# Hymba-style decoder trunk: q and k of the differential attention projected channel-major, rotated rows moved by DMA

## The chip, the cores and the metric

One NeuronCore of a Trainium2 chip runs the kernel. TensorE (PE) does the matrix products, PEld is its weight load, VectorE (DVE), ScalarE (ACT) and GpSimd (POOL) do the rest, SyncE (SP) issues most DMAs. Times are device microseconds; the metric is the median time of a run. Beside the runs there is one execution taken by the profiler, and all rows below come from that one.

## What is computed

Two layers over 512 positions of width 1024, in float32. One projection of the normalised input gives ten parts of 512 columns; four mixers use them, each gated by its own part, and a second projection adds the result to x.

```python
for layer in range(DEPTH):                      # 2
    h = rms_norm(x, norm_g[layer])
    a_u, a_g, qd, kd, vd, b_g, c_x, c_g, m_q, m_g = split(h @ w_in[layer], 10)
    y_a = s5_mixer(a_u, ...)                    # diagonal complex state space, GELU, GLU
    q = rope_partial(qd.reshape(B, L, 4, 2, 64), cos, sin)   # rotates the first 16 of 64
    k = rope_partial(kd.reshape(B, L, 4, 2, 64), cos, sin)
    y_b = rms_norm(diff_attention(q, k, v, lam), da_subln_g[layer]) * (1 - lam_init)
    y_c = rglru_mixer(c_x, ...)                 # convolution of width 4, RG-LRU
    y_m = memory_attention(m_q, rms_norm(mem, mem_norm_g[layer]), w_mem_kv[layer])
    x = x + concat(y_a * silu(a_g), y_b * silu(b_g), y_c * silu(c_g), y_m * silu(m_g)) @ w_out[layer]
return rms_norm(x, final_norm_g)

def rope_partial(x, cos, sin):                  # half = 8
    x1, x2, xp = x[..., :8], x[..., 8:16], x[..., 16:]
    return concatenate([x1 * cos - x2 * sin, x2 * cos + x1 * sin, xp])
```

## The kernel before

Every projection matmul is done in three products of rounded halves: weights and inputs are split into hi and lo (`whi`, `wlo`, `hThi`, `hTlo`), and hi x hi, hi x lo and lo x hi are summed in PSUM. The weights come in pieces of 128 x 1024 by SyncE into two raw buffers; ScalarE casts each to `whi` (line 168) and VectorE subtracts it for `wlo` (line 174), three buffers each, asked for two pieces ahead of their use (`w_use`, line 178).

A projection runs in one of two layouts. `cm_block` (line 502) is channel-major: 256 columns at a time, the result has channels on the partitions and the 512 positions in the row; its matmuls stand at line 515. `tm_block` (line 522) is time-major: 512 columns, positions on the partitions; line 535. Either does 96 matmuls of 512 columns for a 512-column part, and yields after each 12 of them. Accumulators (`acc`) are four PSUM banks; a cm block takes two, a tm block four.

`ORDER` (line 30) gives the order of the projections of each layer. Between them run streams: generators that hold the other work (`params`, `s5_params`, `attention`, `lru`, `s5`, `mem_norm`, `mem_attention` and the ends of these). `Streams.tick` (line 77) is called at each yield of a projection; each stream whose due time has come then emits its next piece and says after how many ticks it is due again. So the program's order is written out by ticks, and it is the order of priority in which each engine takes instructions that are ready. A stream that needs another one polls it each tick.

What bears on the change:

- q and k are time-major. `qk_evac` (line 572) copies a 128-position tile out of PSUM into `qz` (line 575), rotates the first 16 of each 64 columns with four products and two sums on VectorE (`rab`, `qz`), and puts it on the list `pend`. Two ticks later `flush_qk` (line 589) turns it by four TensorE transposes (line 595) and copies it to `qT` (line 598), or for k splits it into `kT` (lines 603 and 604), one for each half of the head pairs, where own rows hold the hi part and the other rows the lo part.
- `attention` (line 608) starts when q, k and v are there (line 1266), `pend` is empty and `par` is done. It works through 16 items, four row blocks times four heads, one each `D_AT` = 2 ticks: scores (lines 645 and 646 on TensorE, the mask, the maximum at line 649, exponentials at line 655, and line 661 on VectorE), a tick pair later the transposes (669), two later the product with v (679). A row block's first item splits q into `qh` and `ql` (lines 629 to 632).
- Buffers come from pools with a fixed count of slots for each size: `big` (`b8`, 8 KB a partition, 14 slots: halves of h, q, the two kT, v, the memory's kv, the LRU's three, `au`, `U`, `yg`, the gates, `qm`), `sm2` (`b2`, 2 KB, 10 slots), `mid` (`b4`, 4 KB, 4 slots). A slot comes free when all uses of its tile are done, and the first write of the next tile waits for that.
- A gate's projection leaves PSUM by `gate_evac` (line 713): a tanh on ScalarE (716) and a product on VectorE (717) that writes the gate's `b8` tile.
- `lru_load` (line 1120) loads and splits the LRU's gate weights when cx is within `BD_AHEAD` entries of the plan; `mem_norm` starts when mk is within `MEM_AHEAD` = 2 entries (line 1151). In the plan a channel-major part has two entries, a time-major one one.
- At the end of a layer `gl` joins the S5 stream (line 1244), and the output projections (`oAM0` and on) join the others.

Of the kernel before, what the change touches and what calls it, by code (L numbers as in the profile page):

```python
# [9 lines left out]
F32 = mybir.dt.float32  # L10
# [6 lines left out]
P = 128  # L17
D = 1024
# [8 lines left out]
ROPE_THETA = 500000.0  # L27


ORDER = ["q v k kv cx au cg bg mq ag mg gl oAM0 oAM1 oBC0 oBC1".split(),  # L30
         "q k cx v kv au mq bg mg ag cg gl oAM0 oAM1 oBC0 oBC1".split()]

C_ID, C_DM, C_IF, C_KEEP, C_CM, C_END = 0, 128, 144, 152, 152, 280

# [13 lines left out]


MEM_AHEAD = 2  # L50
BD_AHEAD = 3
S5P_AT = 2
D_MEM = (3, 2, 1)
D_S5 = (1, 1, 2, 2, 1, 2)
D_AT = 2


class Streams:
# [31 lines left out]
def tile_kernel(ctx: ExitStack, tc: tile.TileContext, A, out):  # L90
# [26 lines left out]
    def b2(shape, name, dtype=F32):  # L117
        return sm2.tile(shape, dtype, tag="b2", name=nm(name))
# [10 lines left out]
    def tp(shape=(P, 4, 128)):  # L129
        return ps.tile(list(shape), F32, tag="tp", bufs=2, name=nm("tp"))  # L130
# [51 lines left out]


    xr = A["x"].rearrange("o (t p) d -> p (o t) d", p=P)
    xd = ctx.enter_context(tc.tile_pool(name="xd", bufs=1, space=bass.MemoryType.DRAM)).tile([L, D], F32, tag="xd", name="xd")
    xdr = xd.rearrange("(t p) d -> p t d", p=P)
    xt = {}

# [32 lines left out]
    for l in range(DEPTH):  # L221
        for n in ORDER[l]:
            if n == "kv":
                for u in range(2):
                    add(l, "mk", u, cm_pieces(A["w_mem_kv"][l], 256 * u))
                add(l, "mv", 0, tm_pieces(A["w_mem_kv"][l], 512))
            elif n == "gl":
                w = A["s5_w_glu"][l].rearrange("(k p) (s c) -> p k s c", p=P, s=2)
                for u in range(2):
                    add(l, "gl", u, [w[:, 2 * i:2 * i + 2, :, 256 * u:256 * u + 256] for i in range(2)])  # L230
            elif n[0] == "o":
                ps_ = []
                for g in n[1:3]:
                    r0 = 512 * "ABCM".index(g)
                    ps_ += tm_pieces(w_out[l, r0:r0 + 512], 512 * int(n[3]))
                add(l, "o", n[1:], ps_)
            elif n in ("q", "k", "v", "au"):
                add(l, n, 0, tm_pieces(w_in[l], COL[n]))
            else:
                for u in range(2):  # L240
                    add(l, n, u, cm_pieces(w_in[l], COL[n] + 256 * u))
# [107 lines left out]
    def tt(o, a, b, op):  # L349
        V.tensor_tensor(out=o, in0=a, in1=b, op=op)  # L350
# [63 lines left out]
    def params():  # L414
# [71 lines left out]
        V.tensor_scalar(out=cneg, in0=cpos, scalar1=-4.0, scalar2=None, op0=ALU.mult)  # L486
        V.tensor_scalar(out=cpos, in0=cpos, scalar1=4.0, scalar2=None, op0=ALU.mult)

    nsum = const.tile([P, NT], F32, tag="nsum", name="nsum")

    mrs = const.tile([P, 2], F32, tag="mrs", name="mrs")
# [77 lines left out]
        return ((lambda k, t: hi[k // 4][:, k % 4, t, :]), (lambda k, t: lo[k // 4][:, k % 4, t, :]))  # L569


    def qk_evac(dst):
        def f(t, a):
            z = b2([P, 8, 64], "qz")
            S.copy(z, a.rearrange("p (m d) -> p m d", d=64))
            z12 = z[:, :, 0:16].rearrange("p m (s f) -> p m s f", f=8)
            ca = rcos[:, t, :].unsqueeze(1).unsqueeze(1).to_broadcast([P, 8, 2, 8])
            sa = rsin[:, t, :].unsqueeze(1).unsqueeze(1).to_broadcast([P, 8, 2, 8])
            rab = b2([P, 2, 8, 2, 8], "rab")
            ra, rb = rab[:, 0], rab[:, 1]  # L580
            tt(ra, z12, ca, ALU.mult)
            tt(rb, z12, sa, ALU.mult)
            tt(z12[:, :, 0, :], ra[:, :, 0, :], rb[:, :, 1, :], ALU.subtract)
            tt(z12[:, :, 1, :], ra[:, :, 1, :], rb[:, :, 0, :], ALU.add)
            pend.append((dst, t, z, st.now))
        return f

    pend = []
    def flush_qk():

        while pend and st.now - pend[0][3] >= 2:
            dst, t, z, _ = pend.pop(0)
            pt = tp()
            for j in range(4):
                PE.transpose(pt[:, j, :], z[:, 2 * j:2 * j + 2, :].rearrange("p m d -> p (m d)"), ident)
            ts = slice(t * 128, (t + 1) * 128)
            if len(dst) == 1:
                S.copy(dst[0][:, :, ts], pt)
            else:

                for m in range(2):
                    own, oth = slice(m * 64, m * 64 + 64), slice(64 - m * 64, 128 - m * 64)
                    S.copy(dst[m][own, :, ts], pt[own])
                    tt(dst[m][oth, :, ts], pt[own], dst[m][own, :, ts], ALU.subtract)

    st.hook = flush_qk

    def attention(l, R):
        while pend or "par" in st.live:
            yield  # L610
        qT, kT, v = R["qT"][0], R["kT"], R["v"]
        o = qT
        R["o"] = o
        oss = const.tile([P, 16], F32, tag="oss", name=nm("oss"))
# [530 lines left out]
        st.start("s5p", s5_params(l, Rl[l]))  # L1145

    st.start("par", params())
    s5p_start(0)
    for pi, (l, n, u, ids) in enumerate(plan):
        R = Rl[l]  # L1150
# [5 lines left out]
        if any(p[0] == l and p[1] == "cx" for p in plan[pi:pi + BD_AHEAD]) and "bd" not in R:  # L1156
            lru_load(l, R)
        if n in ("q", "k"):
            R[n + "T"] = [b8([P, 4, L], "qT")] if n == "q" else [b8([P, 4, L], "kT", F32R) for _ in range(2)]
            run(tm_block(h_tm(), qk_evac(R[n + "T"]), ids))  # L1160
        elif n == "v":
            vt = R["v"] = b8([P, NT, 512], "v")

# [78 lines left out]
        elif n == "gl":  # L1242
# [4 lines left out]
            for hf, pid in enumerate(ids):  # L1247
                whi, wlo = (w.rearrange("p (k s c) -> p k s c", k=2, s=2) for w in w_use(pid))
                for j in range(2):
# [13 lines left out]
                        ag = R["ag"][:, 2 * u + j, :]  # L1263
                        V.scalar_tensor_tensor(out=ag, in0=th, scalar=0.25, in1=ag, op0=ALU.mult, op1=ALU.mult)
                    st.tick()
        if n in ("q", "k", "v") and all(a in R for a in ("qT", "kT", "v")):
            st.start("attn", attention(l, R))
        if n == "o":
            pair, half = u[:2], int(u[2])
# [99 lines left out]
```

## Time and profile before

| | before |
|---|---|
| median of 3 runs | 910.19 us (909.8 to 910.3) |
| the profiled execution | 911.01 us |
| its span, first to last instruction | 909.2 us |
| TensorE matmul busy | 887.7 us, 98% |
| TensorE weight load busy | 746.5 us, 82% |
| VectorE busy | 667.3 us, 73% |
| ScalarE busy | 510.7 us, 56% |
| GpSimd busy | 42.2 us, 5% |
| HBM read | 84.40 MB |

Busy times are unions of an engine's instructions. Matmuls overlap, so the distance from one start to the next says more than the duration of one. "Idle before" is the time an engine waited ahead of an instruction, with the one that ended the wait.

### The profile page before, as it was taken

How to read it: one execution, taken by the hardware profiler on the slowest of the kernel's cores; microseconds unless marked ns; L12 is line 12 of the kernel's file. 1: busy time of each engine (PE TensorE's matmuls, PEld its weight loads, DVE VectorE, ACT ScalarE, POOL GpSimd, SP SyncE). 2: the span in 40 equal slices, each digit the busy share in tenths (PEclk: the TensorE clock that was granted, in tenths of full speed). 3: DMA queues.
4: the chain of work that ended last, by engine and by line, in shares of the span. 5: the costliest groups of instructions: out<-in, count | busy, mean ns of one | idle time of the engine just before them, and what ended most of it. 6: DMA issues, size and time to landing. Idle time of an engine off the chain costs nothing.

```text
span 909.2 us, 12391 instructions
## 1 busy us (share of the span) xinstructions
PE 887.7 (98%) x4478; PEld 746.5 (82%) x4478; DVE 667.3 (73%) x1345; ACT 510.7 (56%) x1032; POOL 42.2 (5%) x86
## 2 busy tenths in 40 slices
PE   7999999999999999999999999999999999999996
PEld 5788878987878888888888888898888888788885
DVE  5984988778999956883384676875999996666343
ACT  5673786985344265921454468766656354863133
POOL 1001000001101100000100000000101110000000
PEclk9999999999999999999999999999999999999998
DMA  5743432022212236433343321432112222152322
GB/s 179 180 139 105 140 95 88 29 68 58 89 55 66 74 115 194 132 107 108 107 157 101 92 88 58 136 116 70 50 48 74 74 74 93 47 186 96 109 73 93
DMA packets 80929, 90.05 MB, mean 99 GB/s; under 512 B 23778, under 2 KB 58211, under 8 KB 80868
## 3 DMA queue, kind: packets, MB, share of 16 engines
q1 hardware_dynamic: 77842, 85.72, 30.1%
q10 hardware_dynamic: 722, 2.36, 0.8%
q0 software_dynamic: 2304, 1.18, 0.5%
q8 instruction: 35, 0.57, 0.3%
q14 instruction: 26, 0.21, 0.1%
HBM read 84.40 MB, written 4.19 MB: 97 GB/s over the span
## 4 chain that ended last, share of the span: by engine, by line
PE 73%; DVE 20%; ACT 5%; issue 2%; DMA 1%; SPq 0%; DVEq 0%; ACTq 0%
PE acc L535 38%; PE acc L515 16%; PE acc L1255 5%; DVE wlo L174 3%; DVE u L350 2%; DVE xr L1040 2%; DVE wt L350 2%; DVE xr L350 1%; PE ms L679 1%; PE tp L315 1%; PE sc L807 1%; PE sc L645 1%; PE tp L832 1%; PE sc L646 1%; DVE li L757 1%
## 5 line engine op out<-in xcount | busy, mean ns | idle before, releaser
L174 DVE TENSOR_TENSOR wlo<-raw,whi 128x1024 fp32r<-128x1024 f32 x136 | 166.0, 1221 | 120.8 <-ACT whi L168 117.0
L168 ACT CAST whi<-raw 128x1024 fp32r<-128x1024 f32 x136 | 143.2, 1053 | 190.4 <-PE acc L535 119.2
L515 PE MATMUL acc<-hThi,whi 128*128 128x512 f32 x384 | 153.3, 399 | 0.0
L515 PE MATMUL acc<-hThi,wlo 128*128 128x512 f32 x384 | 150.8, 393 | 0.0
L515 PE MATMUL acc<-hTlo,whi 128*128 128x512 f32 x384 | 150.6, 392 | 0.0
L535 PE MATMUL acc<-whi,hThi 128*128 128x512 f32 x256 | 104.1, 407 | 2.3 <-ACT whi L168 2.3
L535 PE MATMUL acc<-wlo,hThi 128*128 128x512 f32 x256 | 101.9, 398 | 0.0
L535 PE MATMUL acc<-whi,hTlo 128*128 128x512 f32 x256 | 101.1, 396 | 0.0
L535 PE MATMUL acc<-wlo,mxh 128*128 128x512 f32 x256 | 100.1, 391 | 0.0
L535 PE MATMUL acc<-whi,mxl 128*128 128x512 f32 x256 | 100.1, 391 | 0.0
L535 PE MATMUL acc<-whi,mxh 128*128 128x512 f32 x256 | 100.0, 391 | 0.0
L515 PEld LDWEIGHTS acc<-hThi,wlo 128*128 128x128 f32 x384 | 72.2, 188 | 14.8
L515 PEld LDWEIGHTS acc<-hTlo,whi 128*128 128x128 f32 x384 | 72.3, 188 | 13.3
L515 PEld LDWEIGHTS acc<-hThi,whi 128*128 128x128 f32 x384 | 72.2, 188 | 13.3
L535 PEld LDWEIGHTS acc<-whi,hThi 128*128 128x128 f32 x256 | 56.3, 220 | 10.3 <-ACT whi L168 2.7
L535 PEld LDWEIGHTS acc<-whi,hTlo 128*128 128x128 f32 x256 | 56.5, 221 | 7.8 <-DVE hTlo L318 0.2
L535 PEld LDWEIGHTS acc<-wlo,hThi 128*128 128x128 f32 x256 | 56.5, 221 | 7.2
L535 PEld LDWEIGHTS acc<-wlo,mxh 128*128 128x128 f32 x256 | 48.1, 188 | 9.8
L535 PEld LDWEIGHTS acc<-whi,mxl 128*128 128x128 f32 x256 | 48.1, 188 | 9.8
L535 PEld LDWEIGHTS acc<-whi,mxh 128*128 128x128 f32 x256 | 48.1, 188 | 9.6
L976 POOL DMA_DIRECT2D MT<-kq x64 | 32.1, 509 | 486.2 <-DVE kq L350 336.6
L655 ACT ACTIVATE e<-sc,nmx 128x128 f32<-128x128 f32 (+3 forms) x64 | 33.2, 528 | 10.3 <-DVE nmx L651 10.2
(313 smaller groups left out, 1643.1 us busy)
## 6 DMA issues: line engine op xcount, KB each, us to landing
raw<-in_w_in_dram SPq DMA_DIRECT2D x80, 512.0 KB, 3.6
raw<-in_w_out_dram SPq DMA_DIRECT2D x32, 512.0 KB, 3.4
raw<-in_w_mem_kv_dram SPq DMA_DIRECT2D x16, 512.0 KB, 3.3
x<-in_x_dram SPq DMA_DIRECT2D x8, 512.0 KB, 4.9
raw<-in_s_w_glu_dram SPq DMA_DIRECT2D x16, 256.0 KB, 3.2
mt<-in_mem_dram SPq DMA_DIRECT2D x4, 512.0 KB
xd<-x SPq DMA_DIRECT2D x4, 512.0 KB, 4.4
x<-xd SPq DMA_DIRECT2D x4, 512.0 KB, 5.5
```

The lines of the kernel that those rows point to most:

```text
L168: S.copy(hi, wbuf[j])
L174: V.tensor_tensor(out=lo, in0=raw, in1=hi, op=ALU.subtract)
L315: lastins["pe"] = PE.transpose(pt[:, k, :], h[:, kk * 128:(kk + 1) * 128], ident)
L350: V.tensor_tensor(out=o, in0=a, in1=b, op=op)
L515: PE.matmul(a[j][:, :ncol], w[:, kk, c], h(k), start=(hf == 0 and i == 0), stop=(hf == 1 and i == 3 * nh - 1))
L535: PE.matmul(a[t], h(k, t), w[:, kk, :], start=(p == 0 and kk == 0 and i == 0), stop=(p == np_ - 1 and kk == 1 and i == 2))
L645: PE.matmul(s[:, m, :M], qh[:, m, h, :], kT[m][:, h, :M], start=True, stop=False)
L646: PE.matmul(s[:, m, :M], ql[:, m, h, :], kT[m][:, h, :M], start=False, stop=True)
L655: S.activation(e[:, m, :N], s[:, m, :N], AF.Exp, bias=nmx[:, m:m + 1], scale=0.125, accum_out=sm[:, m:m + 1])
L976: G.dma_start(out=MT[g * 64 + 64 - n:g * 64 + 64, g, t], in_=kq[g * 64:g * 64 + n])
L1040: V.tensor_tensor_scan(out=xr_[i][:, j, :], data0=dec, data1=xr_[i][:, j, :], initial=0.0, op0=ALU.mult, op1=ALU.add)
L1255: PE.matmul(a, w[:, k, s, j * 128:(j + 1) * 128], h[:, 2 * hf + k, :], start=(hf == 0 and i == 0), stop=(hf == 1 and i == 5))
```

## The change

q and k are projected channel-major by `cm_block`, like the gates, and copied from PSUM as they are; no transposes follow. Their layout then has the 16 rotated channels of a 64-channel half on 16 partitions, for four head pairs. A new stream `rope` moves these rows by two DMAs of 128 KB into a tile of 128 partitions, where the two members of each rotated pair lie 32 partitions apart, rotates them with four products on 32 partitions and two instructions on 128, and moves them back by two DMAs. For k it then splits the tile into the two `kT`. The cosines and sines are needed in that layout too: `rope_tables` spreads them with eight GpSimd copies, turns them with eight TensorE transposes once, keeps them for layer 0 and stores them to DRAM, from where layer 1 loads them. k goes ahead of q in both layers, v ahead of both, and cx between k and q in layer 1. `attention` now waits for the streams `ropeq` and `ropek` and is started when q's projection ends; q's tile becomes its output tile as before. `D_ROPE` holds the ticks between the moves out and the rotation, and between the moves back and what follows, for each tensor and layer. `BD_AHEAD` goes from 3 to 1.

```diff
@@ -27,8 +27,8 @@
 ROPE_THETA = 500000.0
-ORDER = ["q v k kv cx au cg bg mq ag mg gl oAM0 oAM1 oBC0 oBC1".split(),
-         "q k cx v kv au mq bg mg ag cg gl oAM0 oAM1 oBC0 oBC1".split()]
+ORDER = ["v k q kv cx au cg bg mq ag mg gl oAM0 oAM1 oBC0 oBC1".split(),
+         "v k cx q kv au mq bg mg ag cg gl oAM0 oAM1 oBC0 oBC1".split()]
 C_ID, C_DM, C_IF, C_KEEP, C_CM, C_END = 0, 128, 144, 152, 152, 280
@@ -48,11 +48,12 @@
 MEM_AHEAD = 2
-BD_AHEAD = 3
+BD_AHEAD = 1
 S5P_AT = 2
 D_MEM = (3, 2, 1)
 D_S5 = (1, 1, 2, 2, 1, 2)
 D_AT = 2
+D_ROPE = {"k": ((2, 3), (2, 3)), "q": ((4, 6), (3, 5))}
 class Streams:
@@ -182,7 +183,8 @@
     xr = A["x"].rearrange("o (t p) d -> p (o t) d", p=P)
-    xd = ctx.enter_context(tc.tile_pool(name="xd", bufs=1, space=bass.MemoryType.DRAM)).tile([L, D], F32, tag="xd", name="xd")
+    dpool = ctx.enter_context(tc.tile_pool(name="xd", bufs=1, space=bass.MemoryType.DRAM))
+    xd = dpool.tile([L, D], F32, tag="xd", name="xd")
     xdr = xd.rearrange("(t p) d -> p t d", p=P)
     xt = {}
@@ -234,7 +236,7 @@
                     r0 = 512 * "ABCM".index(g)
                     ps_ += tm_pieces(w_out[l, r0:r0 + 512], 512 * int(n[3]))
                 add(l, "o", n[1:], ps_)
-            elif n in ("q", "k", "v", "au"):
+            elif n in ("v", "au"):
                 add(l, n, 0, tm_pieces(w_in[l], COL[n]))
             else:
                 for u in range(2):
@@ -486,6 +488,32 @@
         V.tensor_scalar(out=cneg, in0=cpos, scalar1=-4.0, scalar2=None, op0=ALU.mult)
         V.tensor_scalar(out=cpos, in0=cpos, scalar1=4.0, scalar2=None, op0=ALU.mult)
+    rtab = []
+    rtd = [dpool.tile([P, L], F32, tag=f"rtd{i}", name=f"rtd{i}") for i in range(2)]
+    def rope_tables():
+        for w, src in enumerate((rcos, rsin)):
+            rep_ = b2([P, NT, P], "rep")
+            for i in range(NT):
+                G.tensor_copy(rep_[:, i].rearrange("p (a f c) -> p a f c", a=4, c=4),
+                              src[:, i].unsqueeze(1).unsqueeze(3).to_broadcast([P, 4, 8, 4]))
+            yield 2
+            pr = tp()
+            for i in range(NT):
+                PE.transpose(pr[:, i, :], rep_[:, i], ident)
+            pf = pr.rearrange("p i c -> p (i c)")
+            tab = b2([P, L], f"rt{w}")
+            if w == 0:
+                S.copy(tab, pf)
+            else:
+                for g in range(4):
+                    r = slice(g * 32, g * 32 + 32)
+                    S.activation(tab[r], pf[r], AF.Copy, scale=-1.0 if g % 2 else 1.0)
+            rtab.append(tab)
+            G.dma_start(out=rtd[w], in_=tab)
     nsum = const.tile([P, NT], F32, tag="nsum", name="nsum")
     mrs = const.tile([P, 2], F32, tag="mrs", name="mrs")
@@ -569,46 +597,45 @@
         return ((lambda k, t: hi[k // 4][:, k % 4, t, :]), (lambda k, t: lo[k // 4][:, k % 4, t, :]))
-    def qk_evac(dst):
-        def f(t, a):
-            z = b2([P, 8, 64], "qz")
-            S.copy(z, a.rearrange("p (m d) -> p m d", d=64))
-            z12 = z[:, :, 0:16].rearrange("p m (s f) -> p m s f", f=8)
-            ca = rcos[:, t, :].unsqueeze(1).unsqueeze(1).to_broadcast([P, 8, 2, 8])
-            sa = rsin[:, t, :].unsqueeze(1).unsqueeze(1).to_broadcast([P, 8, 2, 8])
-            rab = b2([P, 2, 8, 2, 8], "rab")
-            ra, rb = rab[:, 0], rab[:, 1]
-            tt(ra, z12, ca, ALU.mult)
-            tt(rb, z12, sa, ALU.mult)
-            tt(z12[:, :, 0, :], ra[:, :, 0, :], rb[:, :, 1, :], ALU.subtract)
-            tt(z12[:, :, 1, :], ra[:, :, 1, :], rb[:, :, 0, :], ALU.add)
-            pend.append((dst, t, z, st.now))
-        return f
-    pend = []
-    def flush_qk():
-        while pend and st.now - pend[0][3] >= 2:
-            dst, t, z, _ = pend.pop(0)
-            pt = tp()
-            for j in range(4):
-                PE.transpose(pt[:, j, :], z[:, 2 * j:2 * j + 2, :].rearrange("p m d -> p (m d)"), ident)
-            ts = slice(t * 128, (t + 1) * 128)
-            if len(dst) == 1:
-                S.copy(dst[0][:, :, ts], pt)
-            else:
+    def rope(l, R, n):
+        z = R[n + "z"]
+        while "rtab" in st.live:
+            yield
+        if l and n == "k":
+            rtab[:] = [b2([P, L], f"rt{i}") for i in range(2)]
+            for w in range(2):
+                S.dma_start(out=rtab[w], in_=rtd[w])
+        x1, x2 = b2([P, L], "rx"), b2([P, L], "ry")
+        rows = [(x1[m * 64:m * 64 + 64], z[m * 64:m * 64 + 16]) for m in range(2)]
+        for x_, z_ in rows:
+            S.dma_start(out=x_, in_=z_)
+        yield D_ROPE[n][l][0]
+        co, si = rtab
+        for g in range(4):
+            to, fr = slice(g * 32, g * 32 + 32), slice((g ^ 1) * 32, (g ^ 1) * 32 + 32)
+            tt(x2[to], x1[fr], si[fr], ALU.mult)
+        tt(x1, x1, co, ALU.mult)
+        tt(x1, x1, x2, ALU.add)
+        for x_, z_ in rows:
+            G.dma_start(out=z_, in_=x_)
+        yield D_ROPE[n][l][1]
+        if n == "k":
+            kT = R["kT"] = [b8([P, 4, L], "kT", F32R) for _ in range(2)]
+            for h in range(0, 4, 2):
+                hs = slice(h, h + 2)
                 for m in range(2):
                     own, oth = slice(m * 64, m * 64 + 64), slice(64 - m * 64, 128 - m * 64)
-                    S.copy(dst[m][own, :, ts], pt[own])
-                    tt(dst[m][oth, :, ts], pt[own], dst[m][own, :, ts], ALU.subtract)
-    st.hook = flush_qk
+                    S.copy(kT[m][own, hs], z[own, hs])
+                    tt(kT[m][oth, hs], z[own, hs], kT[m][own, hs], ALU.subtract)
+                yield
     def attention(l, R):
-        while pend or "par" in st.live:
+        while any(n in st.live for n in ("par", "ropeq", "ropek")):
             yield
-        qT, kT, v = R["qT"][0], R["kT"], R["v"]
+        qT, kT, v = R["qz"], R["kT"], R["v"]
         o = qT
         R["o"] = o
         oss = const.tile([P, 16], F32, tag="oss", name=nm("oss"))
@@ -1145,6 +1172,7 @@
         st.start("s5p", s5_params(l, Rl[l]))
     st.start("par", params())
+    st.start("rtab", rope_tables())
     s5p_start(0)
     for pi, (l, n, u, ids) in enumerate(plan):
         R = Rl[l]
@@ -1156,8 +1184,15 @@
         if any(p[0] == l and p[1] == "cx" for p in plan[pi:pi + BD_AHEAD]) and "bd" not in R:
             lru_load(l, R)
         if n in ("q", "k"):
-            R[n + "T"] = [b8([P, 4, L], "qT")] if n == "q" else [b8([P, 4, L], "kT", F32R) for _ in range(2)]
-            run(tm_block(h_tm(), qk_evac(R[n + "T"]), ids))
+            if u == 0:
+                R[n + "z"] = b8([P, 4, L], n + "z")
+            zt = R[n + "z"]
+            def z_evac(j, a, u=u, zt=zt):
+                S.copy(zt[:, 2 * u + j, :], a)
+            run(cm_block(h_cm(), 8, z_evac, ids))
+            if u == 1:
+                st.start("rope" + n, rope(l, R, n))
         elif n == "v":
             vt = R["v"] = b8([P, NT, 512], "v")
@@ -1263,7 +1298,7 @@
                         ag = R["ag"][:, 2 * u + j, :]
                         V.scalar_tensor_tensor(out=ag, in0=th, scalar=0.25, in1=ag, op0=ALU.mult, op1=ALU.mult)
                     st.tick()
-        if n in ("q", "k", "v") and all(a in R for a in ("qT", "kT", "v")):
+        if n == "q" and u == 1:
             st.start("attn", attention(l, R))
         if n == "o":
             pair, half = u[:2], int(u[2])
```

## Rows read from the trace of the kernel before

**Rows 1.** The page: engine totals, and the ended-last chain by engine.

```profile
PE 887.7 (98%) x4478; PEld 746.5 (82%) x4478; DVE 667.3 (73%) x1345; ACT 510.7 (56%) x1032; POOL 42.2 (5%) x86
...
PE 73%; DVE 20%; ACT 5%; issue 2%; DMA 1%; SPq 0%; DVEq 0%; ACTq 0%
```

**Rows 2.** Stretches: length; busy PE, PEld, DVE, ACT, POOL; granted clock, DMA share, GB/s.

```profile
89.00:147.00 58.00, 57.62 (x329) 48.12 (x328) 50.56 (x103) 45.47 (x110) 0.78 (x2) 1.00 0.36 113
...
220.00:307.00 87.00, 85.27 (x461) 72.48 (x461) 86.01 (x167) 32.92 (x67) 12.01 (x24) 1.00 0.23 70
...
563.00:621.00 58.00, 56.99 (x320) 52.51 (x319) 45.69 (x90) 39.60 (x104) 0.00 (x0) 1.00 0.37 118
...
655.00:692.00 37.00, 36.58 (x218) 31.52 (x217) 36.70 (x73) 17.95 (x43) 4.01 (x8) 1.00 0.20 60
692.00:753.00 61.00, 60.85 (x342) 52.17 (x341) 60.17 (x120) 29.60 (x60) 8.01 (x16) 1.00 0.21 64
```

**Rows 3.** Timeline of TensorE, 38 to 47 us: start, us, instruction, idle before.

```profile
38.71 0.39 PE L535 MATMUL acc<-whi,hTlo 128*128 128x512 f32 x1
39.49 0.63 PE L595 MATMUL tp<-cst,qz 128*128 128x128 f32 x4 [0.39 <-DVE rden L350]
41.44 0.63 PE L595 MATMUL tp<-cst,qz 128*128 128x128 f32 x4 [1.32 <-DVE tA L350]
41.82 0.48 PE L535 MATMUL acc<-whi,hThi 128*128 128x512 f32 x1
...
44.41 0.39 PE L535 MATMUL acc<-whi,hTlo 128*128 128x512 f32 x1
44.64 1.03 PE L595 MATMUL tp<-cst,qz 128*128 128x128 f32 x8
45.43 0.48 PE L535 MATMUL acc<-whi,hThi 128*128 128x512 f32 x1
45.75 0.40 PE L535 MATMUL acc<-wlo,hThi 128*128 128x512 f32 x1
```

**Rows 4.** Groups by shape: count, busy us, mean ns, idle before.

```profile
L350 DVE TENSOR_TENSOR ql<-qT,qh 64x512 fp32r<-64x512 f32 x32 | 21.9, 684 | 0.5
...
L649 DVE TENSOR_REDUCE mx<-sc 128x2 f32<-128x1024 f32 x8 | 9.7, 1217 | 0.1
...
L595 PE MATMUL tp<-cst,qz 128*128 128x128 f32 x64 | 8.9, 274 | 2.1 <-DVE tA L350 1.3 <-DVE rden L350 0.4 <-DVE kT L350 0.4
...
L661 DVE SCALAR_TENSOR_TENSOR e<-e,cc 128x512 f32<-128x512 f32 x8 | 6.0, 746 | 0.1
...
L350 DVE TENSOR_TENSOR rab<-qz,cs 128x128 f32<-128x128 f32 x16 | 4.6, 287 | 3.8 <-ACT qz L575 3.8
```

**Rows 5.** Groups of GpSimd.

```profile
L1123 POOL MEMSET bd<- 128x512 f32 x4 | 2.1, 526 | 214.7 <-DVE tab L350 166.9 <-PE tp L885 26.6 <-DVE qz L350 21.2
```

**Rows 6.** DMA issues: count, KB each, median us to landing.

```profile
B<-in_s_b_re_dram SPq DMA_DIRECT2D x4, 128.0 KB, 5.2
```

**Rows 7.** Timelines, layer 0 (190 to 209 us) and layer 1 (625 to 700).

```profile
196.51 0.39 PE L646 MATMUL sc<-kT,ql 128*128 128x512 f32 x1
...
198.19 1.07 ACT L929 COPY U<-tp 128x512 f32<-128x512 f32 x2
...
637.36 0.60 PE L928 MATMUL tp<-cst,au 128*128 128x128 f32 x4
...
638.27 1.27 DVE L350 TENSOR_TENSOR qm<-acc,qm 128x512 fp32r<-128x512 f32 x2
```

**Rows 8.** Timelines of TensorE and VectorE, layer 1, around the gate bg.

```profile
667.72 0.40 PE L646 MATMUL sc<-kT,ql 128*128 128x512 f32 x1
...
674.04 0.68 DVE L717 SCALAR_TENSOR_TENSOR bg<-th,acc 128x512 f32<-128x512 f32 x1
```

**Rows 9.** Timeline of VectorE, layer 1: maxima of two neighbouring score items.

```profile
663.81 1.19 DVE L649 TENSOR_REDUCE mx<-sc 128x2 f32<-128x1024 f32 x1
...
675.90 1.22 DVE L649 TENSOR_REDUCE mx<-sc 128x2 f32<-128x1024 f32 x1
```

## Prediction, made before the changed kernel was run

> **What bounds the kernel now.** I read the page's engine totals first, then the table of stretches, then single stretches in order of time. TensorE is busy for 98% of the span, the chain that ended last lies 73% on TensorE and 20% on VectorE [rows 1]. A busy share alone says little, since a matmul is written down with some 0.39 us while the next starts 0.23 us after it; the pace is what counts, and in the plain projection blocks TensorE holds it: 512 columns every 0.23 us, with the clock granted at 1.00, the 2.4 GHz level [rows 2, 3]. So nearly every instruction taken from TensorE is worth its pace, where nothing else comes last. Something else comes last in two stretches: from 220 to 307 us (layer 0) VectorE is busy for 86.0 of 87 us, from 655 to 753 us (layer 1) for 36.7 of 37 and 60.2 of 61 [rows 2]. There the S5 steps, the gates and the end of the attention meet. Before them VectorE has room: 50.6 of 58 us from 89 to 147, 45.7 of 58 from 563 to 621.
>
> I count in steps. A step is what the kernel emits between two ticks of its streams, 12 matmuls in most blocks, 12 x 0.23 = 2.7 us; numbered from a layer's start, q, k and v end at 24 in layer 0; the memory keys and values take 12 steps, every other projection 8, for the diff keeps all these lengths.
>
> **The change part by part.**
>
> *Transposes out.* 64 transposes of q and k go. Eight cost 45.75 - 44.41 = 1.34 us less two matmul paces (0.46), so 0.88 us, 0.11 each [rows 3]: 64 x 0.11 = 7.0 us off TensorE. Their own mean is 0.274 us [rows 4], but they overlap. The Trainium skill ("TensorE: Matmul & The Clock Gate", Part 4) prices one transpose in a kernel at about 275 ns; the row has the same duration, but another starts every 0.11 us, and by that price the saving would be 17.6 us instead of 7.0. I keep the pace; the other is a rival.
>
> *Transposes in.* The rotation tables take 8 transposes once: +0.9 us.
>
> *The first block.* From 38.71 to 41.82 us TensorE does one matmul (0.23) and 8 transposes (0.88), so 2.0 us are waiting, for VectorE's parameter work [rows 3]. These transposes go, but the table transposes take their place: they need the same sines, and then eight GpSimd copies. No copy stands on GpSimd before; the nearest row is its memset of four times the elements, 0.53 us [rows 5], so under 0.53 to some 4 us for eight. I take half back, -1.0 us; ends -2.0 (all back) and +2.0 (a wait as long again). The Trainium skill ("SBUF — State Buffer", "Who interferes with whom") has a VectorE instruction with two SBUF inputs hold up a GpSimd instruction that reads SBUF; that would point to the bad end here, and no run here shows it.
>
> *Vector and scalar work of the rotation.* Per layer and tensor four products on 32 partitions of 512 elements and two on 128 take the place of 16 small ones; a 64-partition instruction of 512 elements is 0.68 us [rows 4], so 6 x 0.68 = 4.1 us; the sixteen of 128 elements and fewer were at most 16 x 0.29 = 4.6 us. The copies of q and k out of PSUM stay 16. I take 0.
>
> *Moves.* Sixteen DMAs of 128 KB, two stores and two loads of 256 KB for the tables. The row of that size is 5.2 us from issue to landing, from HBM [rows 6]. The stream leaves 2 to 6 steps (5.4 to 16 us) for each. ScalarE issues the outward ones right behind its own copies; GpSimd the ones back, where only the S5 moves and the gate weights queue, neither due then. If a landing is late, the key copies wait on ScalarE with the weight casts behind them; 0, end +2.
>
> *The attention starts later.* This is the price. Before, layer 0 starts its scores 2 steps behind k, at step 26, layer 1 one behind v, at 33. After, it needs ropeq: in layer 0 q ends at 24, and 1 + 4 + 6 steps put the first score at 35; in layer 1 q ends at 32, and 1 + 3 + 5 put it at 41. So 9 and 8 steps later, with 32 steps from first to last step of the 18; the S5 steps stay where they are, from 53 on.
> (a) The steps from 24 and 32 on lose attention work where VectorE was at 87% and 79% [rows 2], and small waits with it. -3.0 us for both layers; ends 0 and -5.4 (one step in each layer; TensorE's row shows next to no idle time there, so more can't come back).
> (b) In layer 0 scores 13 to 15 move into the stretch where VectorE has 1 us to spare. One score item at full width is 1.22 + 0.75 + 0.68 = 2.65 us of VectorE without its shorter instructions (0.68: four splits of q for every four items) [rows 4], 8 us for three, while TensorE's part of them (four score matmuls at 0.23, four transposes and four products at 0.11, 1.8 us each, 5.4; the products' pace is an estimate from the transposes') leaves the steps before. +4.0 us; ends 0 and +10.
> (c) In layer 1 a buffer runs out. The pool of 8 KB tiles has 14 slots, and the trace shows that it fills: U is copied at 198.19, right behind the last score matmul at 196.51, when the keys come free; and qm's second half is written at 638.27, behind the last transpose of au from 637.36 [rows 7]. At step 63 of layer 1 there live four halves of h, q, two k, v, two kv, the LRU's output, U, two qm: 14. The gate bg is the fifteenth. Before, the last score matmul is emitted at that same step: it starts at 667.72, and bg's first write follows at 674.04 [rows 8]. After, it is emitted at step 71. bg's four accumulators hold all four banks, so mg's first matmul, at step 68, waits for the keys. 3 to 4 steps of projection, 3.5 x 2.7 = 9.5 us, can't be done meanwhile; TensorE does only stream work. Two items stand between, and two lay 12.1 us apart there [rows 9], so the wait may be as long as 16. VectorE runs on through it, and S5 then ends earlier against the projections: I take +8.0; ends 0 and +16.
> (d) The memory norm starts when kv is within two entries of the plan; q now has two entries, so it starts 4 steps later in both layers, with its transposes right ahead of mk. At most a step each, 5.4: I take +1.5; ends 0 and +5.4.
>
> *BD_AHEAD 3 to 1* loads the gate weights when cx begins; the LRU needs them 9 steps (24 us) on. The work of the projections, now channel-major, is 96 matmuls of 512 columns in both layouts: 0.
>
> **Sum.** -7.0 + 0.9 - 1.0 + 0 - 3.0 + 4.0 + 8.0 + 1.5 = +3.4 us. The profiled execution took 911.0 us (span 909.2 and 1.8 around it): 914.4. The median of the runs is 0.8 under it, so **913.6 us**.
>
> **The rivals.**
> 1. *The late attention is absorbed* (faster). The streams kept to their steps before, and VectorE's free time ahead of the full stretches is larger by what moved. Then (b) and (c) fall away: -8.6, 901.6 us. For it: a slot needs only to be free when TensorE arrives, and step 68 is five behind bg. Against: scores can't run ahead of the projections, which come first on TensorE. 31%.
> 2. *Transposes are worth their duration* (faster): 56 x (0.274 - 0.11) = 9.2 us more than the forecast's, 904.4. The rows at 44.64 to 45.43 speak against it. 4%.
> 3. *Gain and price cancel*, with (c) shorter than the row of two items makes it: within 0.2% of 910.2. 13%.
> 4. *Starved twice* (slower): the held gate's half-results fill the small pool too, and (c) costs 16, (b) 10, (d) 4: +19.9, 930.1 us less what VectorE catches up, some 926. It decides when mg's first matmul stands idle for over 12 us. 10%.
>
> **How the numbers follow.** The forecast has 42%: slower, 912 to 920. With rival 4, slower has 52%; rivals 1 and 2 make 35% faster; 13% stay within 0.2%, about what a measurement of this kernel can tell from no change. The range for 8 in 10 goes from 901 (rival 1) to 926.
>
> **What would show it.** Transposes right: no line-595 transposes, TensorE's instruction count down by 56. (a): VectorE's share between the v/q blocks and au falls. (b): VectorE still full around the gates of layer 0, and the weights' low parts (wlo) on the chain. (c): a hole in the projections at mg's first matmul in layer 1, which ends when bg is written, right behind the last score matmul; without a hole (c) is wrong. (d): mk's first matmul waits for mhi. A first block as long as before would show that the tables took the wait over. If the time is under 905, the late attention cost nothing and rival 1 holds.

## The result and the profile after

| | before | after |
|---|---|---|
| median | 910.25 us (909.80 to 910.79, 4 runs) | 933.15 us (931.04 to 936.05, 4 runs) |
| ratio, 95% interval | | 1.0252, 1.024 to 1.0265 |
| profiled execution, its span | 911.0, 909.2 | 933.4, 931.6 |

The changed kernel is 22.9 us slower. The forecast was 913.6, the range ended at 926. First the page of after, engine totals and the chain by engine, against [rows 1]:

```profile
PE 890.0 (96%) x4422; PEld 745.6 (80%) x4422; DVE 669.7 (72%) x1297; ACT 510.4 (55%) x1021; POOL 50.4 (5%) x104
...
PE 65%; DVE 24%; ACT 6%; issue 2%; DMA 2%; SPq 0%; ACTq 0%; DVEq 0%
```

TensorE has 56 instructions fewer, as the diff says, and yet is busy longer (part of it at a lower clock, see the last section); part of the chain has moved from TensorE to VectorE. The stretches of [rows 2], and a last one from 684 to 710 us (start, end, length; busy PE, PEld, DVE, ACT, POOL; granted clock, DMA share, GB/s):

```profile
89.00:147.00 58.00, 54.44 (x285) 46.87 (x284) 44.17 (x77) 33.49 (x71) 1.03 (x2) 0.97 0.43 125
220.00:307.00 87.00, 86.61 (x483) 73.09 (x483) 86.31 (x168) 42.24 (x96) 12.03 (x24) 1.00 0.20 61
563.00:621.00 58.00, 49.90 (x246) 45.87 (x245) 43.06 (x75) 31.63 (x73) 1.03 (x2) 0.94 0.38 114
655.00:692.00 37.00, 32.72 (x183) 27.24 (x182) 36.71 (x74) 17.11 (x40) 4.00 (x8) 1.00 0.25 74
692.00:753.00 61.00, 52.89 (x272) 43.08 (x271) 49.32 (x97) 29.74 (x67) 4.01 (x8) 0.86 0.12 36
684.00:710.00 26.00, 13.77 (x55) 9.64 (x55) 22.00 (x43) 9.25 (x26) 1.32 (x3) 0.67 0.14 43
```

Layer 0's full stretch is as full as before. Layer 1 has holes, in the steps from 32 on and above all at 684 to 710. The timeline of TensorE there (start, duration, instruction, idle before):

```profile
684.04 0.39 PE L543 MATMUL acc<-hTlo,whi 128*128 128x512 f32 x1
684.27 0.39 PE L543 MATMUL acc<-hThi,wlo 128*128 128x512 f32 x1
...
691.61 0.47 PE L672 MATMUL sc<-kT,qh 128*128 128x512 f32 x1 [2.56 <-DVE u L352]
...
696.99 0.79 PE L672 MATMUL sc<-kT,qh 128*128 128x512 f32 x1 [3.91 <-ACT e L682]
...
707.59 0.77 PE L672 MATMUL sc<-kT,qh 128*128 128x512 f32 x1
708.16 0.63 PE L673 MATMUL sc<-kT,ql 128*128 128x512 f32 x1
708.59 0.63 PE L672 MATMUL sc<-kT,qh 128*128 128x512 f32 x1
709.01 0.56 PE L673 MATMUL sc<-kT,ql 128*128 128x512 f32 x1
709.57 0.50 PE L543 MATMUL acc<-hThi,whi 128*128 128x512 f32 x1
```

And VectorE, which writes bg:

```profile
708.83 2.48 DVE L744 SCALAR_TENSOR_TENSOR bg<-th,acc 128x512 f32<-128x512 f32 x4 [0.43 <-PE sc L673]
```

The last projection matmul of bg starts at 684.27, the first of mg at 709.57, 25.3 us on. Between them stand three score items (691.61, 696.99, 707.59). All four pieces of bg are written at once, from 708.83 on, where before the first came at 674.04 [rows 8]. Of the last item's four score matmuls the second (708.16, and 0.63 long) is the last that reads the first of the two kT: the write starts right behind its end. This is the hole that the prediction described in (c), but not its size.

To see where all the time went I split TensorE's time block by block. For each kind of matmul I took its pace (the lower quartile of the distance from its start to the next start); paces summed are work, the rest of a block is wait. The split is good to some 3 us in a whole kernel.

| us | before | after | after less before |
|---|---|---|---|
| work | 850.7 | 844.6 | -6.1 |
| waits, layer 0 | 23.8 | 25.6 | +1.8: first three blocks -0.3, mv +5.0, the others -2.9 |
| waits, layer 1 | 16.7 | 43.0 | +26.3: bg +18.2, mk +7.0, mv +1.9, ag +1.9, mg -1.5, the others -1.2 |

So the transposes' 6 us did leave TensorE, and 28 us of waiting came: 18 in the hole at bg, 9 in layer 1's memory keys and values and 5 in layer 0's memory values, while the other blocks together wait some 4 us less.

### The profile page after: what moved, and what is told of

Read it like the earlier page. It is cut to its first block, busy times and chain, and to the rows that moved or that the text cites. A ratio compares the mean times of both kernels' runs of the same rounds, so it can differ in the third digit from the quotient of the medians.

```text
span 931.6 us, 12249 instructions
## 1 busy us (share of the span) xinstructions
PE 890.0 (96%) x4422; PEld 745.6 (80%) x4422; DVE 669.7 (72%) x1297; ACT 510.4 (55%) x1021; POOL 50.4 (5%) x104
## 4 chain that ended last, share of the span: by engine, by line
PE 65%; DVE 24%; ACT 6%; issue 2%; DMA 2%; SPq 0%; ACTq 0%; DVEq 0%
PE acc L563 29%; PE acc L543 21%; PE acc L1290 5%; DVE wlo L175 3%; DVE u L352 3%; DVE xr L1067 2%; DVE wt L352 2%; DVE xr L352 1%; DVE xp L352 1%; DVE mx L676 1%; ACT whi L169 1%; PE tp L317 1%; PE ms L706 1%; PE tp L859 1%; DVE tcq L352 1%
## 5 line engine op out<-in xcount | busy, mean ns | idle before, releaser
L543 PE MATMUL acc<-hThi,whi 128*128 128x512 f32 x512 | 203.5, 398 | 0.0
L543 PE MATMUL acc<-hTlo,whi 128*128 128x512 f32 x512 | 201.5, 394 | 0.0
L543 PE MATMUL acc<-hThi,wlo 128*128 128x512 f32 x512 | 201.3, 393 | 0.0
L543 PEld LDWEIGHTS acc<-hThi,wlo 128*128 128x128 f32 x512 | 96.2, 188 | 19.5
L543 PEld LDWEIGHTS acc<-hThi,whi 128*128 128x128 f32 x512 | 96.3, 188 | 18.8 <-DVE bg L744 0.6
L563 PE MATMUL acc<-whi,hThi 128*128 128x512 f32 x128 | 53.4, 417 | 2.4 <-ACT whi L169 2.4
L563 PE MATMUL acc<-wlo,hThi 128*128 128x512 f32 x128 | 51.6, 403 | 0.0
L1003 POOL DMA_DIRECT2D MT<-kq x64 | 32.1, 509 | 357.2 <-PE tp L1031 184.5
L563 PE MATMUL acc<-whi,hTlo 128*128 128x512 f32 x128 | 51.2, 402 | 0.0
L563 PEld LDWEIGHTS acc<-whi,hThi 128*128 128x128 f32 x128 | 32.3, 252 | 5.8 <-ACT whi L169 2.8
L563 PEld LDWEIGHTS acc<-whi,hTlo 128*128 128x128 f32 x128 | 32.2, 252 | 2.7 <-DVE hTlo L320 0.2
L563 PEld LDWEIGHTS acc<-wlo,hThi 128*128 128x128 f32 x128 | 32.4, 253 | 2.3
```

The lines of the kernel that those rows point to most:

```text
L543: PE.matmul(a[j][:, :ncol], w[:, kk, c], h(k), start=(hf == 0 and i == 0), stop=(hf == 1 and i == 3 * nh - 1))
L563: PE.matmul(a[t], h(k, t), w[:, kk, :], start=(p == 0 and kk == 0 and i == 0), stop=(p == np_ - 1 and kk == 1 and i == 2))
L1003: G.dma_start(out=MT[g * 64 + 64 - n:g * 64 + 64, g, t], in_=kq[g * 64:g * 64 + n])
```

## The experiments

**Is it the slots?** Two kernels. In the first, the kernel before only has its attention of layer 1 held for eight steps:

```diff
+        for _ in range(8 if l == 1 else 0):
+            yield
```

> The kernel before, its q and k time-major and turned on TensorE as ever; only the attention of layer 1 is held back 8 more steps before its first score. Slots theory: the late attention alone keeps the keys, bg finds no tile of 8 KB, and TensorE stands ahead of mg's first matmul as in the changed kernel: a hole of 20 to 25 us there, 925 to 932 us in all. Rival (the new layout, its moves and 32-partition products make the hole): no hole, 910 to 914 us.

926.82 us (two runs), 1.0183 (1.0163 to 1.0203). Lateness alone, in the old layout, makes the hole. Its stretch 655 to 692, and its bg:

```profile
655.00:692.00 37.00, 28.76 (x152) 23.02 (x150) 36.04 (x74) 16.51 (x40) 4.01 (x8) 0.89 0.20 60
...
702.27 2.48 DVE L719 SCALAR_TENSOR_TENSOR bg<-th,acc 128x512 f32<-128x512 f32 x4 [0.43 <-PE sc L648]
```

The second is the kernel after with two 8 KB tiles fewer alive in layer 1 (the low halves of kv and qm are written over the high halves):

```diff
-                R["kv"] = [b8([P, 2048], "kv", F32R) for _ in range(2)]
+                R["kv"] = [b8([P, 2048], "kv", F32R) for _ in range(2 - l)] * (1 + l)
-                R["qm"] = [b8([P, 4, L], "qm", F32R) for _ in range(2)]
+                R["qm"] = [b8([P, 4, L], "qm", F32R) for _ in range(2 - l)] * (1 + l)
```

> The changed kernel; in layer 1 the low halves of kv and of qm are written over the high halves, so two tiles of 8 KB fewer are alive (the memory attention of layer 1 then multiplies wrong low parts); the instructions, their sizes and their order in the program are the same. Slots theory: bg and yg find tiles at once, the 25 us hole ahead of mg in layer 1 is gone, and part of the wait at the memory's keys and values with it: 908 to 916 us. Rival (VectorE, busy for 14.9 of 15 us inside the hole, is what TensorE waits for): the time stays within 3 us of the changed kernel's 933 and the hole is only spread.

910.77 us, 1.0002 (0.9991 to 1.0012): 22.4 us come back. The same stretches:

```profile
655.00:692.00 37.00, 36.95 (x203) 31.08 (x202) 36.44 (x73) 19.82 (x44) 4.01 (x8) 1.00 0.24 74
692.00:753.00 61.00, 60.33 (x352) 50.82 (x352) 57.59 (x115) 35.75 (x85) 7.69 (x16) 1.00 0.17 55
```

VectorE is as full as before (36.4 of 37 us) and TensorE has no hole. VectorE's load alone makes no hole; the missing slots make it. The wait at mk fell too, from 8.4 to 1.3.

**How large is it for each step?** The kernel after with q's rotation in layer 1 given 2 and 2 steps, not 3 and 5:

```diff
-D_ROPE = {"k": ((2, 3), (2, 3)), "q": ((4, 6), (3, 5))}
+D_ROPE = {"k": ((2, 3), (2, 3)), "q": ((4, 6), (2, 2))}
```

> The kernel after; only layer 1's rotation of q gets 2 and 2 steps instead of 3 and 5, so that its attention starts four steps sooner and its last score is emitted at step 67, not 71. Slots theory: of the three items that stand in the hole two come ahead of it, and the hole shrinks from 25 to about 8 us: 933.2 - 17 = 916, 911 to 921. If it is VectorE's load around the gates that makes the hole, four steps change little: 928 to 933. If two steps are too few for the moves, attention waits for them where it starts, and some 5 us of the gain are lost: 921.

923.01 us, 1.0142 (1.0127 to 1.0157): 10.1 us less, not 17. TensorE around the hole, and VectorE's first piece of bg:

```profile
688.93 0.39 PE L543 MATMUL acc<-hThi,wlo 128*128 128x512 f32 x1
...
695.52 0.47 PE L672 MATMUL sc<-kT,qh 128*128 128x512 f32 x1 [3.57 <-DVE u L352]
...
698.20 0.79 PE L543 MATMUL acc<-hThi,whi 128*128 128x512 f32 x1 [1.51 <-DVE bg L744]
...
697.49 1.26 DVE L744 SCALAR_TENSOR_TENSOR bg<-th,acc 128x512 f32<-128x512 f32 x2
```

The hole itself shrank as expected, from 25.3 to 9.3 us (688.93 to 698.20), with one score item in it (695.52) instead of three; the first piece of bg comes 11.3 us sooner (708.83 - 697.49). The time followed by 10.1 us only, 2.5 for each of the four steps: by the split the wait at bg fell by 11.7 us, the rest of the 16 was work that TensorE did inside the hole and now does elsewhere, and the wait at mg rose by 3.7. And one thing does not fit a count by steps. The last score is now emitted at step 67, ahead of mg's first matmul at step 68, and still its item stands in the hole: items run behind the step at which they are emitted.

**Other orders of the gates.** Layer 1 in the order of layer 0, so that cg and bg are written before mq:

```diff
-         "v k cx q kv au mq bg mg ag cg gl oAM0 oAM1 oBC0 oBC1".split()]
+         "v k q kv cx au cg bg mq ag mg gl oAM0 oAM1 oBC0 oBC1".split()]
```

> The changed kernel with layer 1's projections in layer 0's order (v k q kv cx au cg bg mq ag mg gl), all else the same. Attention and S5 meet on VectorE as before, but bg's step finds 13 tiles of 8 KB alive and not 14. Slots theory: no hole of 25 us at the gates, 905 to 914 us, perhaps a few us under the kernel before. Rival (VectorE's crowding is the cost): 925 to 935 us.

914.78 us, 1.0049 (1.0031 to 1.0068). No hole at bg (wait 1.3); the memory attention runs into the output projections, whose first block is 32.3 us long against 21.8. And with the two gates ahead of mq (`v k cx q kv au bg ag mq mg cg gl`):

> The kernel after, with the order of layer 1 changed behind au: bg, ag, mq, mg, cg instead of mq, bg, mg, ag, cg. The two gates then take the 13th and 14th slot, and mq's two halves, the 15th and 16th tile, are first written at step 72, behind the last score of step 71. Slots theory: no hole, as with two slots free: 911, 908 to 914, with the hole in the memory's keys (6 to 8 us) left as it is, since it lies ahead of the change. If the memory attention, which then starts at step 84 instead of 76, runs into the output projections as it does in the order of layer 0, some 4 us more: 915. If it is VectorE's load that makes the hole, it comes back at mq: 925 to 933.

915.58 us, 1.0066 (1.0045 to 1.0086). Again no hole at bg; the wait in mk stayed at 8.4.

**Is the lateness in layer 0 paid for?** The kernel before, attention of layer 0 held for nine steps (the edit of the first run, with `9 if l == 0`):

> The kernel before with the attention of layer 0 alone held back 9 steps. Slots theory: in layer 0 no tile is missing at the gates, so lateness costs only VectorE's crowding there: 909 to 914 us, no hole. Rival (lateness as such costs, by S5 and attention meeting on VectorE): 20 us as in layer 1, 925 to 932 us.

910.22 us, 1.0001 (0.9991 to 1.0012). It costs nothing, and brings nothing.

**What is a transpose worth?** The kernel before, with each flush's four transposes done twice:

```diff
-            for j in range(4):
-                PE.transpose(pt[:, j, :], ...)
+            for _ in range(2):
+                for j in range(4):
+                    PE.transpose(pt[:, j, :], ...)
```

> The kernel before, with the four transposes of each flush of q and k done twice: 64 transposes more on TensorE, nothing else. If a transpose costs its pace, 64 x 0.11 = 7.0 us: 917.3. If it costs its duration, 64 x 0.274 = 17.5 us: 927.8. If the transposes lie in time in which TensorE waits anyway, 0 to 2 us: 910 to 912; then taking them out could bring no more than that either.

916.32 us, 1.0065 (1.005 to 1.008): 5.9 us for 64, 0.09 each. One group in its timeline, sixteen where eight stood in [rows 3]:

```profile
44.27 1.91 PE L596 MATMUL tp<-cst,qz 128*128 128x128 f32 x16
```

**The wait at layer 1's memory keys.** The run with the gates first, and cx right behind v in layer 1 (`v cx k q kv au bg ag mq mg cg gl`), so that the LRU gives its slots back sooner:

> As the run with the gates first, and in layer 1 cx stands right behind v, so that the LRU begins eight steps sooner; attention begins at the same step, 41. If the hole of 8.4 us in layer 1's memory keys is the wait for the slots that the LRU gives back, it falls to 1 us or less: 915.6 - 7.5 = 908, 906 to 911. If it comes from VectorE's or the DMAs' load in those steps instead, the hole stays and the time is 914 to 917.

911.47 us, 1.0013 (1.0004 to 1.0022), 4.1 less than with the gates first. The stretch 565 to 579, of the run with the gates first, and then of this one:

```profile
565.00:579.00 14.00, 6.05 (x35) 5.19 (x34) 13.86 (x20) 4.42 (x7) 1.03 (x2) 0.82 0.47 131
```

```profile
565.00:579.00 14.00, 12.05 (x89) 11.18 (x87) 9.20 (x14) 6.06 (x10) 1.03 (x2) 1.00 0.51 157
```

The wait in mk fell from 8.4 to 1.9: it was the LRU's slots, as the run with two slots free says too. The opposite in layer 0, cx ahead of the memory's keys, on top of the run with the gates first (`v k q cx kv au cg bg mq ag mg gl`):

> As the run with the gates first, and in layer 0 cx now stands ahead of the memory's keys and values, so that attention (from step 35 on) runs beside them. If the hole of 5.6 us in layer 0's memory values is the weight stream, which falls behind where TensorE has nothing but half-width work, attention beside it gives the stream its time, and the hole falls under 2 us: 4 us under the run with the gates first. If the memory's keys then wait for a slot instead, as those of layer 1 do, the hole only moves: 0 to +5 against that run.

933.01 us, 1.0246 (1.0229 to 1.0263). The wait in mv fell to 2.2, but 23.3 us stand in mk. By my count there is again a fifteenth tile here (the LRU's three, the memory norm's two and kv's two among them); that this is the cause was not tried by itself.

**The wait in layer 0's memory values.** Here the weights come last. The kernel after without the two DMAs that move q's rotated rows back in layer 0 (its attention then reads q unrotated):

```diff
-        for x_, z_ in rows:
+        for x_, z_ in rows if (l, n) != (0, "q") else []:
             G.dma_start(out=z_, in_=x_)
```

> The kernel after, without the two DMAs that move layer 0's rotated rows of q back (attention of layer 0 then reads q unrotated); all else stays, the moves out and the rotation among it. In the kernel after, two weight pieces of the memory values are cast 6.5 and 5.7 us after their issue, the ones before them 3.5; the moves back are issued between. If these moves hold the weight stream up, both come at 3.5, the hole in layer 0's memory values falls from 5.6 to 1 us or less, and the time by 5: 928. If the stream is simply too slow for half-width work, as I read it so far, the hole stays at 5 to 6 us, and the time at 932 to 934.

933.33 us, as slow as the kernel after. But the hole went, from 5.6 to 1.0 us; the six kernels that share the layer 0 of the kernel after, itself among them, have 5.2 to 7.0 here. The casts of two weight pieces, the memory's last and cx's first, start 5.0 and 3.6 us after the pieces' issue, not 6.5 and 5.7. ScalarE's longest waits for them from 85 to 117 us (us, times, longest), and the load of the memory's last piece (start, us to landing), of after and then of this run:

```profile
ACT whi L169 <- DMA raw<-in_w_mem_kv_dram: 10.2, 4, 5.0
...
101.14 6.37 DMA raw<-in_w_mem_kv_dram
```

```profile
ACT whi L169 <- DMA raw<-in_w_mem_kv_dram: 5.7, 2, 3.8
...
103.08 4.95 DMA raw<-in_w_mem_kv_dram
```

So the moves do hold the weight loads up, and my first reading (a stream too slow for half-width work) falls. Yet the 4.6 us didn't reach the end: cx took 2.2 and cg 2.0 more, and 1.9 more stood in q, ahead of anything that the edit touches, where the kernels with this layer 0 spread from 2.1 to 4.0. The run that was to use it, cx early with the memory sooner (below) and 9 and 2 steps for q in layer 0:

> As the run with the memory sooner, with 9 and 2 steps instead of 4 and 6 for q in layer 0: the moves back then fall behind the memory's last weights, into cx, and attention begins one step later. If the moves back make the hole, it is gone: 911.4 - 3 to 5 = 907, 905 to 909. If two steps are too few for them, TensorE waits at attention's first scores (ScalarE's splits) by some 3 us: 909 to 912. If the stream alone makes the hole: 911 to 913.

914.43 us, 1.0045 (1.0032 to 1.0059). It did not do what I meant: the moves back were issued at 104.19 us, 1.8 behind the issue of the memory's last piece (102.37) where it was 1.2 in the kernel after, so they still ran beside its load. That load took 6.7 us to land, and the wait in mv stayed (4.5). The run does not tell the two readings apart.

**Looking for a faster one.** On top of cx early: q's rotation in 2 and 2 steps in both layers; the memory norm started within 3 entries, not 2; and this with mg ahead of mq in layer 1 and the memory attention started when mq ends.

> As the run with cx early, and q's rotation gets 2 and 2 steps in both layers (4 and 6, 3 and 5 before), so that attention begins six steps sooner in layer 0 and four in layer 1. If the holes in the memory values (5.2 us in layer 0, 2.6 in layer 1) are the weight stream, which falls behind where TensorE has no attention to do, the first falls to some 2 us and the second to 1: 4 to 5 us under the run with cx early, 903 to 905. If the moves need more than two steps, attention's first splits hold ScalarE up, and with it the weight casts: no gain, or up to 5 us more.

917.70 us, 1.0082 (1.0066 to 1.0098). The waits in the memory values stayed (6.9 and 3.2 us), and TensorE's wait for the first split of q in layer 0 rose from 2.2 to 4.0. The rest of the 6.2 us was not followed up.

> As the run with cx early, and the memory norm starts within three entries of the plan instead of two: eight steps ahead of mk again, as in the kernel before, instead of four. If the 2 us that TensorE stands still ahead of the norm's transposes in layer 0 (and up to 1.9 in layer 1's keys) are its lateness, they go: 911.5 - 3 = 908.5, 907 to 910. If VectorE's work is merely moved to another wait, nothing changes: 911 to 912.

911.43 us, 1.0003 (0.9994 to 1.0012). The wait in layer 1's mk fell from 1.9 to 0, its mv's rose from 3.1 to 4.9.

> As the run with the memory sooner, and layer 1's order behind au is bg, mg, mq, ag, cg instead of bg, ag, mq, mg, cg, with the memory attention started at the end of mq (step 76 instead of 84). It then no longer runs into the output projections, whose first block was 25.0 against 21.8 us: some 3 us less than the run with the memory sooner, 905 to 906. If the memory attention and the end of S5 crowd VectorE instead, as much comes back in ag and cg: no change, or 2 us more.

911.28 us, 1.0006 (0.9995 to 1.0017). The output projections are free again (21.8 us), and cg has 36.8 us instead of 32.1. None of the versions is faster than the kernel before.

## Why the prediction was wrong

- **Transposes out, -7.0: right.** 56 instructions fewer, 6.1 us less work, and 5.9 us when they are doubled. Rival 2 falls. The Trainium skill ("TensorE: Matmul & The Clock Gate", Part 4) gives about 275 ns for one; as a duration the traces agree (0.27), as a price they do not (0.09).
- **Tables and first block, -0.1 together: right in size.** The first block waits 3.2 us where it waited 5.4. The eight GpSimd copies took 3.1 us, inside the bound; their groups in the profile of after (count, busy, mean ns, idle before):

```profile
L500 POOL COPY rep<-sn 128x128 f32<-128x128 f32 x4 | 2.0, 550 | 0.0
...
L500 POOL COPY rep<-cs 128x128 f32<-128x128 f32 x4 | 1.1, 310 | 28.6 <-DVE pl L482 28.6
```

  Seven of the eight took 0.29 to 0.33 us and one 1.28, which makes the mean of its group 550; TensorE waited for none. The Trainium skill ("SBUF — State Buffer", "Who interferes with whom") has VectorE instructions with two SBUF inputs hold up a GpSimd instruction that reads SBUF, which would fit the long one; no run here tells whether it is that.
- **Vector and scalar work, 0: near.** VectorE is busy 2.4 us longer than before, ScalarE 0.3 us less.
- **Moves, 0: the wrong thing was checked.** I looked at what queues behind them and when they are due, not at what else the DMAs carry. Beside the moves back two weight pieces come some 2 us later each, and layer 0's memory values wait 5 us more.
- **(a), -3.0: nothing came back.** With only layer 1's attention held in the kernel before, the waits from mk to mq do fall, from 6.1 to 3.0 us by the split. In the kernel after the weights (layer 0) and the slots (layer 1) came last there instead, and the waits rose.
- **(b), +4.0: zero.** The held attention in layer 0 shows it, together with that layer's part of (a), which is at most 1 us by the split. In the kernel after bg and mq are 5.2 and 7.5 us longer, and the blocks ahead of them are shorter by as much: work changed its block, and TensorE stays full (86.6 of 87 us).
- **(c), +8.0: the right mechanism, mis-sized.** This step failed: bg's block waits 18.2 us longer than before. I took items to run at the step where they are emitted, which leaves two behind mg's first matmul, and priced 3.5 steps at 2.7 us. With VectorE full they run behind their step, so three stood in the hole instead of two, and they came 5.4 and 10.6 us apart. The run with the rotation sooner separates the two: four steps are worth 10.1 us, 2.5 each, so the price of a step was near right; but where the count by steps leaves no hole at all, an item still stands in one, and by the split bg and mg together wait 8.7 us longer than before. That backlog, put at nothing, is the missing part: with 3.5 steps at 2.5 it makes 17.5 (an estimate), where bg's 18.2 less mg's 1.5 are 16.7. The rows of before had it: the last item's scores are done by 668.1, and VectorE takes their maximum at 675.90 [rows 8, 9]. Besides, nothing was given back: I had VectorE finish S5 sooner, but the blocks of gates behind the hole together wait 0.9 us longer than before, not less. Rival 4 named 12 us of standing as its point of decision; it was 25, with (b) and (d) not as it said, and whether the small pool filled, its reason, no run shows.
- **(d), +1.5: within its ends.** TensorE waits 1.8 us for the memory norm in layer 0, ahead of the norm's transposes and not at mk's first matmul, which waits for nothing; starting it sooner gained nothing in the end.
- **Not in the sum: layer 1's memory keys, +7.0.** I counted the slots at step 63 only. At steps 32 to 40 four halves of h, q, two kT, v, the LRU's three and the memory norm's two make 13, and kv needs two. Before, the LRU's last scan starts at 570.09; after, at 576.43, while the projections come 4.7 us sooner. VectorE there in the kernel after:

```profile
568.42 2.77 DVE L352 TENSOR_TENSOR ry<-rx,rt 32x512 f32<-32x512 f32 x4
...
576.43 1.22 DVE L784 TENSOR_TENSOR_SCAN li<-lr,xc 128x512 f32<-128x512 f32 x1
577.68 1.42 DVE L352 TENSOR_TENSOR kv<-acc,kv 128x256 fp32r<-128x256 f32 x4
```

  The rotation of q (`ry`, and two of `rx`) stands between the LRU's last instructions, and kv's low half is first written right behind the last scan.
- **A count in the text** is off without effect: attention's 18 pieces span 17 gaps of 2, 34 steps, not 32. The last score at step 71 is right.

One thing stays open. In the kernels without the large holes TensorE's work is 6 to 10 us less than before (the split is good to 3) and the time is the same: their waits are 48.6 (memory sooner) to 52.5 us (cx early) against 40.5. The largest stand in the memory's values of both layers (3.5 and 4.9 with the memory sooner, against 0.6 and 0.9). Part is the weights behind the moves, but taking layer 0's moves away moved the wait on. What would let the gain through was not found.

## What to carry to other kernels

When a consumer is moved later, count the live tiles of each pool at every step where a new one is asked for, not at one step, and name who stands behind the first write that must wait. Price lateness by the steps and, on top, by the backlog of the engine that the late work runs on: here the steps were worth 2.5 us each, near the 2.7 of the bare matmuls, and some 8 us more came from items that ran behind their step. Work taken from the fullest engine pays only if no stream of loads or slots is nearly as late there: here 6 us of transposes were saved and 28 us of waiting came.

## What the runs showed of the hardware

Two DMAs of 128 KB between SBUF tiles, issued between two weight loads of 512 KB (101.14 and 104.14 us), went with casts that start 6.5 and 5.7 us after the loads' issue, against 3.5 for the two loads before them; without the two DMAs it was 5.0 and 3.6. These are single executions.

In the hole TensorE ran at the lower of its levels, 1.2 GHz. Two stretches of the kernel after, in the columns of [rows 2]:

```profile
685.00:692.00 7.00, 3.08 (x22) 2.63 (x23) 7.00 (x14) 0.86 (x1) 0.32 (x1) 1.00 0.51 156
693.00:709.00 16.00, 8.02 (x26) 6.10 (x26) 12.00 (x26) 7.00 (x20) 0.00 (x0) 0.50 0.00 0
```

The granted clock was still 1.00 where TensorE was busy for 3.1 of 7 us, and 0.50 in the 16 us behind it. The last score matmuls start 0.42 to 0.57 us apart, where two of them stood 0.23 apart at the hole's beginning (691.92 and 692.15), so that the item which the hole waits for was itself slower by about 1 us.
